# Seven places for split weights, and the first stick-breaking head loaded through ScalarE's queue

## The chip, the cores and the metric

The kernel runs on one core of one Trainium2 chip. The metric is device time in microseconds (us). TensorE (PE) multiplies, VectorE (DVE), ScalarE (ACT) and GpSimd (POOL) do the elementwise work, and SyncE (SP) issues nearly all DMAs. "PEld" is PE's weight load, which the profile lists apart from the matmul.

## The reference, cut to what matters

One layer of a hybrid encoder is computed for 1024 prompt tokens and 32 streaming tokens (with 512 cached positions), model width 1024, all in float32:

```python
z = einsum(rmsnorm(x), w_in)            # q/k/v of mixers A and B, indexer, two gates
o_a = softmax over the 256 best keys    # mixer A: 8 heads of 64, top-k by a small indexer
a   = exp(log_sigmoid(z) - tail)        # mixer B: stick-breaking, strictly causal, 8 heads of 64
m   = sigmoid(gate_a) * (o_a @ w_branch_a) + sigmoid(gate_b) * (o_b @ w_branch_b)
h   = x + m @ w_out
y   = h + relu(rmsnorm(h) @ w_up)**2 @ w_down
```

The new keys and values of both mixers are outputs too.

## The kernel before, in words

**Split numbers.** A float32 product is made of three matmuls of the type fp32r: each operand is split into a high part and the rest, and `three` issues high by high, high by rest, rest by high. A weight block of 128x512 is a *unit*: SP loads it into one of three places `wst`, ACT rounds it into `wh` (a CAST), and POOL or DVE subtracts to get `wl`. The pairs `wh0/wl0`, `wh1/wl1` and so on are the *places for split weights*; `unit` and, in the feed-forward part, `form` take them in turn (`self.place = (self.place + 1) % WB`). A place can be written again only when PE has read the unit that was in it before.

**Stages.** (1) RMS norm and the indexer's projections; (2) the projections of mixer B (`project_b`) and the indexer's scores, with the top-k search by bits on DVE and ACT beside them; (3) the projections of mixer A (`project_a`): for each of four pairs of heads a value part, whose columns go to bank `pj`, are scaled by DVE into `vt` and transposed by PE, and a query/key part, nine tiles of tokens in banks `s` and `pj`, which DVE rotates; (4) stick-breaking attention, eight heads (`attend(h, False)`); (5) softmax attention in two passes; (6) merge, output projection and feed-forward network (a Strassen scheme), from about 890 us on to the end.

**One head of stick-breaking attention.** `attend` loads k, q and v from DRAM, where the projections left them. For each of eight tiles of 128 queries it multiplies k and q into a bank `s` (three of them), ACT takes two sigmoids of it (`p` and `rem`), DVE scans `rem`, POOL multiplies `p` by it, PE transposes `p` into a bank `t` (two), ACT and DVE split that into `tt`, and PE multiplies `tt` by v into a bank `o`.

**What sets the order.** Nothing is issued in the order in which it is written. Every operation is recorded, and a planner (`Plan`) plays them through with a table of costs: an engine that falls free takes the operation of the best rank whose inputs are there by these costs, and the order thus found is fixed for each engine. The ranks are FAST (evictions), PREP (loads and splits), MAIN, FILL and SLOW. Matmuls of weights have rank FILL (`with nc.rank(FILL)`): the projections of the gates and, later, of the branches are there to fill PE while attention waits for ACT, DVE and POOL. On the chip each engine runs its list in order and waits by semaphores. Operations recorded as `nc.either` go to DVE or POOL, whichever the planner finds earlier done. All recorded operations are issued from one line, 440, so groups are told apart by their tiles' names.

**The place of the change.** After `project_a` the pool `att` is opened in the memory of the closed pools, and three gates are recorded before the first head. `nc.tile(pool, shape, type, name, bufs=n)` gives the n places of a name in turn, and a place lies where the pool stands when it is first asked for. So the order of the first requests decides which older tile lies beneath, and what must end before the place is written.

Of the kernel before, what the change touches and what calls it, by code (L numbers as in the profile page):

```python
# [10 lines left out]
F32 = mybir.dt.float32  # L11
F32R = mybir.dt.float32r
# [11 lines left out]
SEQ = 1024  # L24
# [16 lines left out]
LS = PAST + DEC  # L41
W1 = 512
NEW = 8
WB = 5
MIDS = 1
FILL_AHEAD = 1
GATES_BEFORE, GATES_FIRST = 4, 3
# [17 lines left out]
def cut(L):  # L65

    return L // 2 if L in (640, LS) else 512
# [392 lines left out]
class Layer:  # L460
# [21 lines left out]
    def unit(self, src):  # L482
# [5 lines left out]
        with nc.rank(PREP):  # L488
            st = nc.tile(self.wpool, [128, 512], F32, "wst", bufs=3)
            h, l = (nc.tile(self.wpool, [128, 512], F32R, f"{z}{self.place}") for z in ("wh", "wl"))  # L490
            self.place = (self.place + 1) % WB
            nc.sync.dma_start(st, src)
# [71 lines left out]
    def run(self):  # L564
        nc, a = self.nc, self.a
# [12 lines left out]
        w = lambda *x: [nc.tile(self.wpool, [128, 512], F32R, name) for name in x] and None  # L578
# [11 lines left out]
        w("wh3", "wl3")  # L590
        self.fq = s([128, NT, H], "fq")
        w("wh4", "wl4")
        with nc.rank(PREP):
            nc.scalar.dma_start(self.gm, a["g_mix"])
        nc.vector.memset(self.rs, 1.0)
# [4 lines left out]
        dt = lambda shape, name: nc.tile(self.dram, shape, F32, name)  # L600
# [62 lines left out]
        self.low = nc.either  # L663
        self.att = self.pr = nc.open("att", "right")
        self.first = nc.tile(self.att, [128, T], U8, "first")
        nc.gpsimd.memset(self.first[:, DEC:SEQ + DEC - 128], 0)
        nc.scalar.copy(self.first[:, :DEC], self.eye4)
        nc.scalar.copy(self.first[:, SEQ + DEC - 128:], self.ident)
# [405 lines left out]
            nc.sync.dma_start(self.fqs[32 * j:32 * j + 32], self.fq[:DEC, NEW, j::4])  # L1074


    def rope_tables(self):
        nc, a, pr = self.nc, self.a, self.pr
        self.tc_ = nc.tile(pr, [128, NT, 2, HD], F32, "tabc")
        self.ts_ = nc.tile(pr, [128, NT, 2, HD], F32, "tabs")  # L1080
        C = nc.tile(pr, [128, NT, HD], F32, "ropec")
        S = nc.tile(pr, [128, NT, HD], F32, "ropes")
        g = nc.tile(pr, [128, 2, HD], F32, "gqk")
        nc.sync.dma_start(C, a["rope_c"])
        nc.sync.dma_start(S, a["rope_s"])
        nc.sync.dma_start(g, a["g_qk"].unsqueeze(0).to_broadcast([128, 2, HD]))
        for j in range(2):
            nc.gpsimd.tensor_mul(self.tc_[:, :, j], C, g[:, j].unsqueeze(1).to_broadcast([128, NT, HD]))
            gx = g[:, j].rearrange("p (s e) -> p s e", s=2)[:, ::-1, :].unsqueeze(1).to_broadcast([128, NT, 2, 32])
            nc.gpsimd.tensor_mul(  # L1090
                self.ts_[:, :, j].rearrange("p t (s e) -> p t s e", s=2),
                S.rearrange("p t (s e) -> p t s e", s=2), gx)
# [161 lines left out]
    def attend(self, h, is_a, passes=(0, 1)):  # L1254

        nc, at = self.nc, self.att
        g = h if is_a else H + h
        direct = is_a and passes[0] == 1 and h >= H - 2
        if direct and h == H - 2:
            self.last = nc.tile(at, [128, SEQ], F32, "last", tag="v", bufs=3)  # L1260
        kk = nc.tile(at, [128, SEQ], F32R, "k", bufs=3)
        v = nc.tile(at, [128, 8, 128], F32R, "v", bufs=3)
        dk = self.dk[g].rearrange("s e t -> (s e) t")
        qs = {}
        for i in range(passes[-1] + 1):
            nc.sync.dma_start(kk.bitcast(F32)[:, 512 * i:512 * i + 512], dk[:, 512 * i:512 * i + 512])
            if i in passes:
                qs[i] = nc.tile(at, [128, 2, 512], F32R, "q", bufs=2)
                for s in range(2):
                    nc.sync.dma_start(  # L1270
                        qs[i].bitcast(F32)[HD * s:HD * s + HD],
                        self.dq[g].rearrange("s e t -> e s t")[:, :, 512 * i:512 * i + 512])
            nc.sync.dma_start(v.bitcast(F32)[:, 4 * i:4 * i + 4], self.dv[g, :, 4 * i:4 * i + 4])

        def weights(t, q, *room):
            L = 128 * (t + 1)
            qh, ql = (q[:, s, t % 2 * 128:t % 2 * 128 + 128] for s in range(2))
            parts = []
            for c0 in range(0, L, cut(L)):
                n = min(cut(L), L - c0)  # L1280
                ps = self.bank("s")
                nc.tensor.matmul(ps[:, :n], qh, kk[:, c0:c0 + n], start=True, stop=False)
                nc.tensor.matmul(ps[:, :n], ql, kk[:, c0:c0 + n], start=False, stop=True)
                parts.append((c0, ps[:, :n]))
            if is_a:
                return self.softmax_weights(parts, L, self.mask[t], self.fq[:, t, h:h + 1], room[0])
            return self.stick_weights(parts, L, *room, self.first[:, DEC + SEQ - L:][:, ::-1])

        for i in passes:
            o = nc.tile(at, [64, 512], F32, "o", bufs=2)  # L1290
            for t0 in (4 * i + 2, 4 * i):
                c = 128 * (t0 - 4 * i)
                q = qs[i][:, :, c:c + 256]
                if i:
                    pw = [weights(t, q, *self.rooms(is_a)) for t in (t0, t0 + 1)]
                else:
                    room = self.rooms(is_a)
                    pw = [weights(t0 + j, q, *(z[:, 512 * j:512 * j + 512] for z in room)) for j in range(2)]
                po = self.bank("o")[:, :256]
                for j0 in range(0, t0 + 2, 2):  # L1300
                    pt = self.bank("t")
                    blocks = [(j, u) for j in (j0, j0 + 1) for u in range(2) if j <= t0 + u]
                    for m, (j, u) in enumerate(blocks):
                        nc.tensor.transpose(
                            pt[:, m * 128:m * 128 + 128], pw[u][:, j * 128:j * 128 + 128], self.ident)
                    parts = self.split_pt(pt, 128, 128 * len(blocks))
                    for j in (j0, j0 + 1):
                        lo = 128 if j > t0 else 0
                        s0 = 256 * (j - j0)
                        for z in range(2):  # L1310
                            nc.tensor.matmul(
                                po[:, lo:256], v[:, j], parts[:, z, s0:s0 + 256 - lo],
                                start=j + z == 0, stop=j + z == t0 + 2)
                self.halves(po, o[:, c:c + 256], self.last[h % 2 * HD:h % 2 * HD + HD, c:c + 256] if direct else None)
            if not direct:
                with nc.rank(FAST):
                    nc.sync.dma_start(self.do[g, :, 512 * i:512 * i + 512], o)
            self.mid = self.mid[1:] + [len(nc.nodes) - 1]
# [248 lines left out]
    def ffn(self, rp):  # L1567
# [13 lines left out]
        def form(x, n=512):  # L1581
            with nc.rank(PREP):
                h, l = (nc.tile(self.wpool, [128, 512], F32R, f"{z}{self.place}") for z in ("wh", "wl"))
                self.place = (self.place + 1) % WB
                h, l = h[:, :n], l[:, :n]
# [109 lines left out]
    def down(self, late, form):  # L1695
# [87 lines left out]
        for (fs, weights, after), b, block in (  # L1783
# [4 lines left out]
            total, ask = len(fs) * len(block), iter(range(len(fs) * len(block)))  # L1788
            runs = [block] if len(fs) > 1 else [block[:8], block[8:]]
            for run, q in [(run, q) for run in runs for q in range(4)]:  # L1790
                if q not in banks:
                    tags = [next(self.turn) for _ in fs]
# [130 lines left out]
```

## Time and profile before

| | us |
|---|---|
| three runs | 1676.88, 1678.47, 1678.60 |
| median | 1678.47 |
| the profiled execution's own time | 1679.89 |
| its span, first to last instruction | 1678.1 |
| PE busy in it | 1663.3 (99%) |
| PE loading weights | 1587.8 (95%) |
| DVE, ACT, POOL busy | 1355.1, 945.1, 804.2 |

Matmuls overlap in PE, so each one's duration in the profile is longer than its share of the time: a matmul of 512 columns is listed with about 0.40 us, while the next one starts 0.23 us later. What a matmul costs is the distance between two starts. A number in brackets behind a row, with an arrow, is idle time of the engine just before that row, and who ended it. TensorE's granted clock is 1.00 in every stretch of this section's profile. The chain of waits is PE for 84% of the span.

### The profile page before, as it was taken

How to read it: one execution, taken by the hardware profiler on the slowest of the kernel's cores; microseconds unless marked ns; L12 is line 12 of the kernel's file. 1: busy time of each engine (PE TensorE's matmuls, PEld its weight loads, DVE VectorE, ACT ScalarE, POOL GpSimd, SP SyncE). 2: the span in 40 equal slices, each digit the busy share in tenths (PEclk: the TensorE clock that was granted, in tenths of full speed). 3: DMA queues.
4: the chain of work that ended last, by engine and by line, in shares of the span. 5: the costliest groups of instructions: out<-in, count | busy, mean ns of one | idle time of the engine just before them, and what ended most of it. 6: DMA issues, size and time to landing. Idle time of an engine off the chain costs nothing.

```text
span 1678.1 us, 34748 instructions
## 1 busy us (share of the span) xinstructions
PE 1663.3 (99%) x12244; PEld 1587.8 (95%) x12244; DVE 1355.1 (81%) x2830; ACT 945.1 (56%) x2008; POOL 804.2 (48%) x681
## 2 busy tenths in 40 slices
PE   9999999999999999999999999999999999999999
PEld 9898999899989999998989999999999999999999
DVE  6777899987579889887877649998988997678775
ACT  7556888764366768886665545333333453443431
POOL 4532332344356576354556348544433466345564
PEclk9999999999999999999999999999999999999999
DMA  8243454355573636788764644444444596676674
GB/s 284 61 125 107 142 185 144 99 155 148 163 218 103 181 100 178 190 264 247 227 188 142 178 123 134 157 146 142 142 142 135 198 326 223 204 232 200 222 227 137
DMA packets 182126, 290.31 MB, mean 173 GB/s; under 512 B 29472, under 2 KB 61696, under 8 KB 181920
## 3 DMA queue, kind: packets, MB, share of 16 engines
q1 hardware_dynamic: 181664, 287.91, 55.1%
q8 instruction: 97, 1.59, 0.4%
q14 instruction: 77, 0.63, 0.1%
q10 hardware_dynamic: 288, 0.17, 0.0%
HBM read 195.09 MB, written 94.90 MB: 173 GB/s over the span
## 4 chain that ended last, share of the span: by engine, by line
PE 84%; DVE 7%; DMA 4%; ACT 2%; issue 2%; POOL 1%; SPq 1%; DVEq 0%; ACTq 0%; POOLq 0%
PE pj L440 34%; PE c L440 11%; PE a L440 11%; PE b L440 11%; PE s L440 9%; PE o L440 4%; PE t L440 4%; DVE junk L440 2%; DMA xt<-x 1%; SPq L440 1%; DVE qi L440 0%; DVE y L440 0%; DMA q<-dq 0%; DMA kl<-dc 0%; DVE ta L440 0%
## 5 line engine op out<-in xcount | busy, mean ns | idle before, releaser
L440 PE MATMUL pj<-xl,wh 128*128 128x272 f32 (+2 forms) x1200 | 334.0, 312 | 0.0
L440 POOL TENSOR_TENSOR wl<-wst,wh 128x512 fp32r<-128x512 f32 x125 | 175.4, 1408 | 219.4 <-ACT wh L440 192.9
L440 PE MATMUL pj<-xh,wh 128*128 128x272 f32 (+1 forms) x768 | 251.7, 328 | 0.0
L440 PE MATMUL pj<-xh,wl 128*128 128x272 f32 (+1 forms) x768 | 250.6, 326 | 0.2 <-POOL wl L440 0.2
L440 PEld LDWEIGHTS pj<-xl,wh 128*128 128x128 f32 x1200 | 212.7, 188 | 10.0
L440 ACT CAST wh<-wst 128x512 fp32r<-128x512 f32 x197 | 120.7, 619 | 126.6 <-PE pj L440 35.0
L440 PEld LDWEIGHTS pj<-xh,wl 128*128 128x128 f32 x768 | 144.6, 188 | 10.8 <-POOL wl L440 0.5
L440 PEld LDWEIGHTS pj<-xh,wh 128*128 128x128 f32 x768 | 144.6, 188 | 10.1 <-DVE gz L440 0.3
L440 POOL TENSOR_TENSOR p<-p,rem 128x383 f32<-128x383 f32 (+8 forms) x66 | 107.2, 1639 | 64.7 <-DVE rem L440 31.1
L440 ACT CAST wh<-us 128x512 fp32r<-128x512 f32 x80 | 49.7, 621 | 122.6 <-PE pj L440 34.3
L440 DVE TENSOR_TENSOR tt<-t,tt 128x512 fp32r<-128x512 f32 (+2 forms) x168 | 100.2, 620 | 16.8 <-ACT tt L440 16.0
L440 DVE TENSOR_TENSOR_SCAN rem<-rem,first 128x384 f32<-128x384 f32 (+8 forms) x66 | 107.2, 1642 | 2.0 <-ACT rem L440 1.6
L440 POOL TENSOR_TENSOR wl<-y,wh 128x512 fp32r<-128x512 f32 x46 | 68.6, 1492 | 77.7 <-ACT wh L440 74.7
L440 ACT ACTIVATE junk<-score,cand 128x1024 bf16<-128x1024 f32 (+2 forms) x93 | 96.9, 1042 | 12.5 <-DVE cand L440 11.0
L440 ACT CAST wh<-y 128x512 fp32r<-128x512 f32 x79 | 49.0, 621 | 96.8 <-PE c L440 20.5
L440 ACT CAST tt<-t 128x512 fp32r<-128x512 f32 (+2 forms) x168 | 85.8, 540 | 27.5 <-PE t L440 18.5
L440 PE MATMUL o<-tt,v 128*128 128x256 f32 (+1 forms) x640 | 98.5, 279 | 0.5 <-DVE o L440 0.5
L440 PE MATMUL s<-k,q 128*128 128x512 f32 (+4 forms) x384 | 98.2, 351 | 0.7 <-DMA q<-dq 0.7
L440 PEld LDWEIGHTS o<-tt,v 128*128 128x128 f32 x640 | 90.5, 189 | 6.1 <-DVE o L440 1.1
L440 DVE TENSOR_SCALAR_CACHE_REDUCE junk<-score,cand 128x384 bf16<-128x384 f32 (+1 forms) x124 | 92.9, 749 | 3.1
L440 PE MATMUL t<-ident,p 128*128 128x128 f32 (+1 forms) x596 | 90.7, 275 | 0.0
L440 POOL TENSOR_SCALAR p<-p,nb 128x384 f32<-128x384 f32 (+6 forms) x66 | 53.5, 817 | 70.8 <-DVE nb L440 59.6
(401 smaller groups left out, 5624.3 us busy)
## 6 DMA issues: line engine op xcount, KB each, us to landing
us<-w_down SPq DMA_DIRECT2D x80, 256.0 KB, 3.3
q<-dq SPq DMA_DIRECT2D x64, 256.0 KB, 4.1
du<-us SPq DMA_DIRECT2D x56, 264.0 KB, 2.7
du<-y SPq DMA_DIRECT2D x56, 264.0 KB, 3.0
y<-w_up SPq DMA_DIRECT2D x44, 256.0 KB, 2.8
k<-dk SPq DMA_DIRECT2D x40, 256.0 KB, 4.1
v<-dv SPq DMA_DIRECT2D x40, 256.0 KB, 4.0
xl<-du SPq DMA_DIRECT2D x35, 264.0 KB, 4.7
```

The source lines that it names most:

```text
L440: fn(*args, **kw)
```

## The change

The number of places for split weights goes from five to seven (`WB`), so two more pairs of 128x512 are taken from the pool `w`. When the pool `att` is opened, all places of six of its names are now asked for at once, in a fixed order. And the loads of k, q and v of stick-breaking head 0 (two loads of k, four of q, two of v) are issued by ACT instead of SP.

```diff
-WB = 5
+WB = 7
...
         w("wh4", "wl4")
+        for i in range(5, WB):
+            w(f"wh{i}", f"wl{i}")
...
         self.first = nc.tile(self.att, [128, T], U8, "first")
+        self.places(self.att, [
+            ("gz", [128, 512], F32, 3), ("rem", [128, SEQ], F32, 4), ("tt", [128, 2, 512], F32R, 4),
+            ("v", [128, 8, 128], F32R, 3), ("k", [128, SEQ], F32R, 3), ("q", [128, 2, 512], F32R, 2)])
...
+    def places(self, pool, tags):
+
+        for name, shape, dt, n in tags:
+            for _ in range(n):
+                self.nc.tile(pool, shape, dt, name, bufs=n)
...
         dk = self.dk[g].rearrange("s e t -> (s e) t")
+        load = (nc.sync if h or is_a else nc.scalar).dma_start
         qs = {}
         for i in range(passes[-1] + 1):
-            nc.sync.dma_start(kk.bitcast(F32)[:, 512 * i:512 * i + 512], dk[:, 512 * i:512 * i + 512])
+            load(kk.bitcast(F32)[:, 512 * i:512 * i + 512], dk[:, 512 * i:512 * i + 512])
...
-                    nc.sync.dma_start(
+                    load(
...
-            nc.sync.dma_start(v.bitcast(F32)[:, 4 * i:4 * i + 4], self.dv[g, :, 4 * i:4 * i + 4])
+            load(v.bitcast(F32)[:, 4 * i:4 * i + 4], self.dv[g, :, 4 * i:4 * i + 4])
```

PE has the same 12,235 matmuls in both kernels. Their order is the same up to the 508th, in the index stage, and from there on the planner, which sees more room for units, finds another one on every engine. Three places matter here.

**Start of stick-breaking attention, PE.** `s<-k,q` are the scores of head 0, `t<-ident,p` its transposes, `pj<-..,wh` and `..,wl` the matmuls of gates. Before:

```order
L440 MATMUL s<-k,q 128x384 x2
L440 MATMUL s<-k,q 128x512 x2
L440 MATMUL s<-k,q 128x128 x2
L440 MATMUL pj<-xh_106,wh_4209 128x272
L440 MATMUL pj<-xl_107,wh_4209 128x272
```

Nine gate matmuls stand there, then the scores of the 256-column tile, then nine matmuls of the next gate, and only then the transposes. Now:

```order
L440 MATMUL s<-k,q 128x384 x2
L440 MATMUL s<-k,q 128x512 x2
L440 MATMUL s<-k,q 128x128 x2
L440 MATMUL s<-k,q 128x256 x2
L440 MATMUL s<-k,q 128x512
L440 MATMUL t<-ident,p 128x128 x2
L440 MATMUL s<-k,q 128x512
L440 MATMUL s<-k,q 128x384 x2
L440 MATMUL s<-k,q 128x512 x2
L440 MATMUL t<-ident,p 128x128 x5
L440 MATMUL s<-k,q 128x512 x2
L440 MATMUL o<-tt,v 128x256
```

The gate's last nine matmuls now stand ahead of the first scores, and no gate matmul stands between the first scores and the first product with v.

**The same place, ACT.** Now ACT issues the loads of head 0 in its own list:

```order
L440 CAST first<-ident 128x128
L440 DMA k<-dk 128x512
L440 DMA q<-dq 64x2x512 x2
L440 DMA v<-dv 128x512
L440 ACTIVATE gz<-gz 128x512
L440 DMA k<-dk 128x512
L440 DMA q<-dq 64x2x512 x2
L440 DMA v<-dv 128x512
L440 ACTIVATE gz<-gz 128x272 x2
L440 ACTIVATE p<-s 128x384
```

Before, these eight stood in SP's list, and the two CASTs of the next gate's unit stood right behind the first two sigmoids; now the first such CAST comes behind eleven sigmoids and a CAST of `tt`:

```order
L440 ACTIVATE p<-s 128x512
L440 ACTIVATE rem<-s 128x512
L440 ACTIVATE p<-s 128x384
L440 CAST tt<-t 128x512
L440 CAST wh_6371<-wst 128x512
```

**End of mixer A's projections, PE.** `pj<-xl,wh` with 272 columns are the last value columns of a pair, `t<-ident,vt` their transposes, `pj<-wh,xh` with 256 columns a tile of tokens of the query/key part. Now:

```order
L440 MATMUL pj<-xl_111,wh_4076 128x272
L440 MATMUL pj<-xh_110,wl_4077 128x272
L440 MATMUL t<-ident,vt 128x128 x2
L440 MATMUL t<-ident,vt 32x128
L440 MATMUL pj<-wh_4089,xh_110 128x256
```

and, 24 matmuls later, `t<-ident,qk 128x128 x4` and at once the first `pj` matmul of a gate. Before, the tile of tokens ahead of those four transposes was one of bank `s`, and the transposes of `vt` stood further from the matmuls that make them. So a transpose of `vt` now follows directly on the last matmul whose result DVE scales for it.

**Second pass of softmax attention, PE.** `pj<-og` are matmuls of a branch. Now:

```order
L440 MATMUL t<-ident,p 128x128 x8
L440 MATMUL pj<-og,wl_7521 128x512
L440 MATMUL o<-tt,v 128x256 x5
L440 MATMUL t<-ident,p 128x128 x2
L440 MATMUL o<-tt,v 128x256 x3
L440 MATMUL t<-ident,p 128x128 x5
L440 MATMUL o<-tt,v 128x256 x2
L440 MATMUL o<-tt,v 128x128 x2
```

Before, ten or eight branch matmuls stood between such transposes and their products:

```order
L440 MATMUL t<-ident,p 128x128 x6
L440 MATMUL pj<-og,wh_7497 128x512 x2
L440 MATMUL pj<-og,wl_7498 128x512
L440 MATMUL pj<-og,wh_7497 128x512 x2
L440 MATMUL pj<-og,wl_7498 128x512
L440 MATMUL pj<-og,wh_7497 128x512 x2
L440 MATMUL o<-tt,v 128x256
```

The branch matmuls between transposes and products have shrunk from eight to one, and to none further on.

## The prediction, made before the changed kernel was run

> **What bounds the kernel now.** I read the page's busy times first, then engine busy times by stretch, the waits of ACT by releaser, and last PE's timeline wherever an idle time stands in brackets. In a stretch's row the columns are start and end, length, busy us of PE, PE's weight load, DVE, ACT and POOL with instruction counts, granted clock, DMA share and GB/s.
>
> ```profile
> span 1678.1 us, 34748 instructions
> PE 1663.3 (99%) x12244; PEld 1587.8 (95%) x12244; DVE 1355.1 (81%) x2830; ACT 945.1 (56%) x2008; POOL 804.2 (48%) x681
> ...
> 280.00:425.00 145.00, 142.43 (x1088) 135.35 (x1087) 124.62 (x355) 91.49 (x194) 60.42 (x60) 1.00 0.48 138
> 1040.00:1390.00 350.00, 350.00 (x2877) 350.00 (x2876) 316.70 (x533) 143.87 (x311) 159.74 (x109) 1.00 0.51 175
> ...
> ACT wh L440 <- PE pj L440: 87.0, 57, 4.0
> ACT wh L440 <- PE c L440: 68.7, 43, 2.4
> ```
>
> PE is idle for 1678.1 - 1663.3 = 14.8 us in all. No faster preparation can give back more than that, and the matmuls stay the same. In the feed-forward stretch, 1040 to 1390, PE has no gap at all. The last two rows, the largest of their kind, show what two more places for split weights attack: ACT waits 87.0 and 68.7 us until PE has read the old unit. That is much, but it is ACT's time (56% busy). A unit ready earlier than PE wants it earns nothing. So more places gain only where PE itself waits for a split, and there is little of that. What the change does instead is indirect: the planner finds another order, and the time is set by whether that order still covers the few chains through ACT, DVE and POOL.
>
> **The change part by part.**
>
> *Seven places, in the feed-forward part and the gates' units:* 0. The cover is PE's own work, 350.00 of 350.00 above; the bound below is 0 too, since nothing can be gained there. If the cover were gone, a unit would cost ACT's cast and the subtraction, and that would show as PE behind `wl`.
>
> *Start of stick-breaking attention.* Before, PE looked like this:
>
> ```profile
> 468.70 1.15 PE L440 MATMUL s<-k,q 128*128 128x384 f32 x6
> 469.69 0.34 PE L440 MATMUL pj<-xh,wh 128*128 128x272 f32 x1
> ...
> 470.87 0.40 PE L440 MATMUL s<-k,q 128*128 128x256 f32 x2
> 471.10 0.39 PE L440 MATMUL pj<-xh,wh 128*128 128x512 f32 x1
> ...
> 471.80 0.28 PE L440 MATMUL pj<-xl,wh 128*128 128x272 f32 x1
> 472.32 0.50 PE L440 MATMUL pj<-xh,wl 128*128 128x512 f32 x1 [0.24 <-POOL wl L440]
> ...
> 473.96 0.48 PE L440 MATMUL pj<-xh,wl 128*128 128x512 f32 x1
> 475.18 1.52 PE L440 MATMUL s<-k,q 128*128 128x512 f32 x6 [0.74 <-DMA q<-dq]
> 476.54 0.39 PE L440 MATMUL pj<-xh,wh 128*128 128x512 f32 x1
> ```
>
> Two waits: 472.32 - 471.80 = 0.52 where 0.12 is usual (0.40 lost), and 475.18 - 473.96 = 1.22 where 0.23 is usual (0.99 lost, for the second half of q). Everything else is filled with gate matmuls. In the new order all of the gate's matmuls are ahead of the first score, and up to the first product with v there are only scores and transposes. Their chain, from rows of before:
>
> ```profile
> 469.25 0.49 ACT L440 ACTIVATE p<-s 128x384 f32<-128x384 f32 x1 [1.34 <-PE s L440]
> 469.64 0.49 ACT L440 ACTIVATE rem<-s 128x384 f32<-128x384 f32 x1
> 470.01 1.15 ACT L440 CAST wh<-wst 128x512 fp32r<-128x512 f32 x2
> ...
> 470.23 0.96 DVE L440 TENSOR_TENSOR_SCAN rem<-rem,first 128x384 f32<-128x384 f32 x1 [0.36 <-ACT rem L440]
> ...
> 472.24 1.31 POOL L440 TENSOR_TENSOR p<-p,rem 128x383 f32<-128x383 f32 x1
> ...
> 478.62 0.71 PE L440 MATMUL t<-ident,p 128*128 128x128 f32 x5
> 479.08 0.54 PE L440 MATMUL s<-k,q 128*128 128x320 f32 x2
> ```
>
> The first sigmoid starts 469.25 - 468.70 = 0.55 after the first score, the scan at 470.23 - 468.70 = 1.53 and ends at 2.49. A hand-over takes 0.10 (`rem` ends at 470.13, the scan starts at 470.23). So POOL's product of 1.31 ends at 3.9, and the first transposes start at about 4.0. PE's work ahead of them is 0.99 (469.69 - 468.70, six scores) + 0.23 + 0.23 = 1.45. Then it goes on at the pace of ACT, which reads the banks `s` (three of them) in turn: the second half of the 512-column tile at 4.4, ACT's sigmoids of that tile from 4.6 and 5.1, the next `p` at 5.6, a cast of `tt` at 6.0, and only behind that, in ACT's list, the cast of the next gate's unit, which (1.15 for two, 0.6 for one) lets the first gate matmul start at about 7.2, with `tt` 0.59 ahead of it. PE's work up to there: 0.99 + 0.23 + six scores of 512 1.36 (476.54 - 475.18) + two of 384 0.34 + seven transposes 0.76 (five take 0.46 above with one score's start; 0.109 each by my estimate) + one product 0.12 = 3.8. So PE waits 7.2 - 3.8 = 3.4, and the two old waits (1.4) go: **+2.0**. Bounds: +0.5, if the second tile's scan and product hide fully in the first's (1.5 less), and the upper one under the loads below. A gain here is excluded, since 4.0 - 1.45 = 2.55 up to the first transposes alone is more than 1.4.
>
> *The loads through ACT.* Before, SP issued them, the second half of q behind stores and other loads (a piece of the chain of waits, two of SP's issues, a sigmoid of ACT, a stretch):
>
> ```profile
> 467.89 7.15 DMA q<-dq
> ...
> 466.45 0.42 SPq L440 DMA_DIRECT2D k<-dk  x1
> 466.93 1.57 SPq L440 DMA_DIRECT2D q<-dq  x2
> ...
> 464.72 0.63 ACT L440 ACTIVATE gz<-gz 128x512 f32<-128x512 f32 x1 [4.91 <-DVE gz L440]
> ...
> 466.00:476.00 10.00, 9.03 (x57) 7.76 (x57) 6.28 (x11) 5.13 (x14) 3.53 (x3) 1.00 1.03 319
> ```
>
> ACT is idle 4.91 us ahead of that sigmoid, so issuing the first four loads costs nothing (k 0.42, two of q 1.57, and v at most the 0.79 of a q: 2.8 us). The second four stand behind the sigmoid, which waits for DVE in the new list too. The second q can go out at 464.72 + 0.63 + 0.42 + 0.79 = 466.56, and with the same 7.15 us lands at 473.7 instead of 475.04. The first score now comes 470.87 - 469.69 = 1.18 later, at 469.88; counted from it, that is 3.8, just inside the 4.0 that PE waits anyway. Price: 0 in the sum. If it lands no earlier than before, 475.04 - 469.88 = 5.2, PE waits 1.2 more, which gives the upper bound of +3.2. In that stretch the DMA share is 1.03: the transfers already fill all engines, so an earlier issue need not be an earlier landing.
>
> The Trainium skill, page "DMA: Bandwidth & Descriptors", section "Issuing engines are not separate DMA queues", says that DMAs issued by ScalarE, SyncE and GpSimd run on the same 16 DMA engines and interleave, and that several issuers save only the issue time. The share of 1.03 agrees; by that rule the loads gain at most their place behind SP's other issues, and the sum would be the one with +3.2.
>
> *End of mixer A's projections.* PE's waits of before:
>
> ```profile
> 296.63 0.38 PE L440 MATMUL s<-wh,xh 128*128 128x256 f32 x1 [0.36 <-ACT sq L440]
> ...
> 311.70 0.36 PE L440 MATMUL s<-wh,xh 128*128 128x256 f32 x1 [0.17 <-DVE cand L440]
> ...
> 324.64 0.36 PE L440 MATMUL s<-wh,xh 128*128 128x256 f32 x1 [0.23 <-DVE tb L440]
> ...
> 334.91 0.24 PE L440 MATMUL t<-ident,qk 32*128 32x32 f32 x1 [1.06 <-DVE az L440]
> ...
> 339.50 0.27 PE L440 MATMUL t<-ident,vt 128*32 128x128 f32 x1 [0.23 <-DVE small L440]
> ...
> 415.16 0.38 PE L440 MATMUL s<-wh,xh 128*128 128x256 f32 x1 [0.37 <-ACT wh L440]
> ```
>
> Their brackets sum to 2.4 (PE's whole idle time from 280 to 425 is 145.00 - 142.43 = 2.57); the true loss is some 0.16 more each (as 0.24 against 0.40 above), 3.4. The one of 1.06 stays: its transposes are as close behind their rotation as before. So 2.2 go. New are three transposes of `vt` directly on the last matmul of their columns. And twice a `pj` matmul of 256 columns wants a bank from which DVE has still to read two products. DVE's part:
>
> ```profile
> 467.01 0.44 DVE L440 TENSOR_TENSOR gz<-pj,rb 128x272 f32<-128x272 f32 x1 [2.32 <-PE pj L440]
> ...
> L440 DVE TENSOR_TENSOR ta<-pj,tabc x12: 386/412/425, 298.1 to 432.7; 128x256 f32<-128x256 f32 x12
> ```
>
> A transpose of `vt` waits for the end of a 272-column matmul (0.34 listed), DVE's scaling (0.44, the row's for as many columns, an estimate for `vt`) and the hand-over 0.10, less the usual 0.12: 0.75. A `pj` matmul waits 0.36 + 2 x 0.41 + 0.10 less four transposes (0.44) and 0.12, that is 0.7. New 3 x 0.75 + 2 x 0.7 = 3.6, gone 2.2: **+1.4**. Lower bound +0.2 (DVE's part half hidden: 5 x 0.24 less), upper +3.8 (all five as bad as the worst of before, 1.2 each, less 2.2).
>
> *At about 690 us* ACT's list has two function-table loads ahead of a pair of casts:
>
> ```profile
> L440 ACT ACT_TABLE_LOAD x6 | 7.7, 1283 | 0.1
> ```
>
> Their number is about that of before, but these two, 1.28 each, stand just ahead of a unit that PE wants; nothing in the trace of before shows it. Between 0 (unit ready) and one load, 1.3, I take the middle, **+0.6**.
>
> *Second pass of softmax attention, about 870 us.* Eight transposes have one branch matmul (0.23) behind them, then products:
>
> ```profile
> 847.28 0.52 PE L440 MATMUL s<-kl,qz 128*128 128x272 f32 x2 [0.65 <-POOL kl L440]
> ...
> L440 ACT CAST tt<-t 128x512 fp32r<-128x512 f32 x51 | 29.1, 592 | 7.1 <-PE t L440 5.6
> L440 DVE TENSOR_TENSOR tt<-t,tt 128x512 fp32r<-128x512 f32 x100 | 66.9, 681 | 8.7 <-ACT tt L440 8.1
> ```
>
> ACT's 0.59 and DVE's 0.68 give 1.27 less 0.23, so some 1.0 where nothing else is in flight; then two shorter groups of which half is covered, 0.5 each: 2.0. Against that, the wait for `kl` (0.65, with the 0.16 and a smaller second one about 1.0) goes, since its copy on POOL is now planned earlier: **+1.0**, between 0 (the products are of a tile split earlier) and 2.0 (kl still waits).
>
> **Sum:** 2.0 + 1.4 + 0.6 + 1.0 = +5.0 on the profiled execution's 1679.89 gives 1684.9. That execution is 1.42 above the median of the runs, 1678.47, so the median becomes 1683.5. For places in the new order that I have not priced I add nothing and allow 1.5 either way.
>
> **The rivals.**
> - *Not slower, even faster.* The new order could cover its chains: PE's list puts a transpose or product where the planner's costs have the input ready, and those costs may simply be right. Place: transposes of `vt`, `qk` and the second pass. Point of decision: whether DVE's scaling ends before the matmul ahead of the transpose does. Then the three later terms are -2.2, 0 and -1.0; if also only the first part of the attention's start counts (+0.5), the median is 1678.47 - 2.7 = 1675.8; with the full +2.0, 1677.3. With the start covered as well (against it: no gate matmul stands there) it is 1678.47 - 1.4 - 3.2 = 1673.9. Chance 0.33: 0.10 of faster, 0.23 of within.
> - *The change does not do what it says.* The second half of q lands as late as before, because the transfers share the engines (DMA share 1.03): +1.2, so 1684.7. For it: 7.15 us is the slowest of q's landings. Against: the loads are no longer behind SP's stores. Chance 0.14.
> - *The clock drops.* Every row above has granted clock 1.00. The first matmuls of the program show what cold costs:
>
> ```profile
> 1.19 4.21 PE L440 MATMUL t<-warm 128*128 128x128 f32 x18 [1.19 <-DVE warm L440]
> ```
>
> 0.234 each against 0.109. If 2.5 us of waiting at the start of attention sufficed, some 2.5 us of work behind it would take twice as long: 1686.0. Against: the stretch is broken by scores. Chance 0.05. The Trainium skill, page "TensorE: Matmul & The Clock Gate", section "Part 1: The HAM clock gate", tells of such a gate; the row agrees in kind, and no row here shows a drop once warm.
>
> **How the numbers follow.** The forecast's case has 0.48. A measurement of this kernel can hardly tell less than 0.2%, 3.4 us, from no change: 1675.1 to 1681.8 counts as the same. Of the forecast's case about 0.07 lies under 1681.8 (by the lower bounds 0.5 + 0.2 + 0 + 0, 1679.2). Faster 0.10; same 0.23 + 0.07 = 0.30; slower 0.41 + 0.14 + 0.05 = 0.60. Its own range is 1679 to 1688; with the covered order, whose better half starts at 1675.8, and the upper bounds (3.2 + 3.8 + 1.3 + 2.0 = +10.3, 1688.8, hardly all at once) the range is 1676 to 1689.
>
> **What would show it.** Right: PE idle at the first head's start with releasers `p` on POOL and `s` or `rem` on ACT, 3 us or more between the first score and the first gate matmul not filled; transposes of `vt` waiting 0.6 or more for DVE; a bracket of about 1 behind `tt` near 870; PE's busy time of 1040 to 1390 unchanged. Wrong: PE's total idle time under 15 us, or a wait for q still the largest at that place, or a granted clock under 1.00 near 470, or a difference inside the feed-forward part, where I price nothing.

## The result and the profile after

The changed kernel takes 1699.35 us (median of 4 runs, 1698.70 to 1701.54), the kernel before 1678.40 beside it. The ratio is 1.013 with a 95% interval of 1.0114 to 1.0146: 21 us slower, where +5 was forecast and 1689 was the upper end of the range. The direction was right and the size wrong by a factor of four.

The profiled execution took 1699.98 us, its span is 1696.8, 18.7 more than before. The first lines of its page:

```profile
span 1696.8 us, 34711 instructions
PE 1669.5 (98%) x12244; PEld 1592.2 (94%) x12244; DVE 1369.8 (81%) x2846; ACT 948.0 (56%) x2008; POOL 783.9 (46%) x665
```

PE is idle for 1696.8 - 1669.5 = 27.3 us instead of 14.8, which makes 12.5 of the 18.7. The other 6.2 are PE time: the same 12,244 instructions are busy for 1669.5 instead of 1663.3 us. How they divide was not measured, but the rows show two things. A matmul that stands ahead of a wait counts with its whole listed length, and PE waits more often. And where the granted clock is 0.50 (last section), PE issues 7 matmuls in a us instead of 10.

Busy times by stretch, first of the kernel before, then of the changed one (start and end, length, PE, PE's weight load, DVE, ACT, POOL, granted clock, DMA share, GB/s):

```profile
280.00:440.00 160.00, 157.43 (x1192) 149.18 (x1191) 134.88 (x379) 98.32 (x210) 68.70 (x68) 1.00 0.47 136
440.00:520.00 80.00, 78.73 (x519) 71.67 (x517) 54.21 (x87) 46.17 (x111) 37.12 (x26) 1.00 0.58 170
680.00:840.00 160.00, 159.81 (x1131) 149.02 (x1131) 128.96 (x424) 126.52 (x264) 72.64 (x81) 1.00 0.81 237
840.00:960.00 120.00, 118.96 (x781) 108.66 (x781) 88.20 (x181) 67.55 (x141) 66.81 (x63) 1.00 0.58 169
```

```profile
280.00:440.00 160.00, 153.47 (x1168) 145.72 (x1167) 128.97 (x367) 96.83 (x205) 68.25 (x67) 1.00 0.47 134
440.00:520.00 80.00, 75.77 (x470) 68.16 (x470) 53.10 (x84) 44.00 (x98) 37.92 (x24) 0.96 0.57 166
680.00:840.00 160.00, 157.40 (x1104) 145.67 (x1103) 129.61 (x404) 122.56 (x262) 71.44 (x79) 1.00 0.75 223
840.00:960.00 120.00, 117.06 (x795) 107.70 (x794) 93.23 (x200) 72.75 (x147) 66.76 (x60) 1.00 0.61 186
1040.00:1390.00 350.00, 348.69 (x2856) 347.79 (x2855) 326.24 (x563) 141.34 (x308) 145.39 (x99) 1.00 0.50 170
```

PE's idle time grows from 2.57 to 6.53 us at the end of mixer A's projections, from 1.27 to 4.23 at the start of stick-breaking attention (with a mean clock of 0.96), from 0.19 to 2.60 at the start of softmax attention, from 1.04 to 2.94 behind it. Even the feed-forward stretch has lost 1.31.

The start of attention, PE and ACT of the changed kernel:

```profile
473.80 1.15 PE L440 MATMUL s<-k,q 128*128 128x384 f32 x6
477.73 0.80 PE L440 MATMUL s<-k,q 128*128 128x256 f32 x2 [2.77 <-ACT rem L440]
478.98 0.76 PE L440 MATMUL s<-k,q 128*128 128x512 f32 x1 [0.46 <-ACT rem L440]
480.62 0.69 PE L440 MATMUL t<-ident,p 128*128 128x128 f32 x2 [0.87 <-POOL p L440]
480.96 2.27 PE L440 MATMUL s<-k,q 128*128 128x512 f32 x5
...
485.06 0.50 PE L440 MATMUL pj<-xh,wh 128*128 128x512 f32 x1
```

```profile
465.58 1.32 ACTq L440 DMA_DIRECT2D q<-dq  x2
470.12 0.34 ACTq L440 DMA_DIRECT2D v<-dv  x1
470.50 0.63 ACT L440 ACTIVATE gz<-gz 128x512 f32<-128x512 f32 x1 [5.15 <-DMA q<-dq]
...
471.57 1.81 ACTq L440 DMA_DIRECT2D q<-dq  x2
475.80 0.33 ACTq L440 DMA_DIRECT2D v<-dv  x1
476.17 0.75 ACT L440 ACTIVATE gz<-gz 128x272 f32<-128x272 f32 x2 [5.03 <-DMA q<-dq]
476.82 0.47 ACT L440 ACTIVATE p<-s 128x384 f32<-128x384 f32 x1
```

From the first score to the first gate matmul it is 485.06 - 473.80 = 11.26 us, not 7.2. ACT's first sigmoid starts 3.02 after the first score, not 0.55: it stands in ACT's list behind loads that ACT could not issue. The issue of v waited from 466.9 to 470.12, the last one from 473.4 to 475.80.

The brackets of those rows put both waits down to q. The landings say otherwise: the first two loads of q landed at 472.1 and 472.8, some 2 us after v had gone out. The first v went out 0.1 us behind the landing of a store that SP had issued (`dg<-gz`, issued at 463.74, landed 6.3 us later), the second directly behind the landing of the second k (issued at 471.21, landed 4.6 us later). In the trace each of these two issues waits for the semaphore of that earlier DMA. The bracket of 0.46 has a similar error: the second half of q was issued at 472.80 and landed 6.0 us later, at 478.8, so that the score at 478.98 was held up by q to the end, and not by ACT.

### The profile page after: what moved, and what is told of

It is laid out like the page before. It is cut to its first block, busy times and chain, and to the rows that moved or that the text cites. A ratio compares the mean times of both kernels' runs of the same rounds, so it can differ in the third digit from the quotient of the medians.

```text
span 1696.8 us, 34711 instructions
## 1 busy us (share of the span) xinstructions
PE 1669.5 (98%) x12244; PEld 1592.2 (94%) x12244; DVE 1369.8 (81%) x2846; ACT 948.0 (56%) x2008; POOL 783.9 (46%) x665
## 5 line engine op out<-in xcount | busy, mean ns | idle before, releaser
L440 POOL TENSOR_TENSOR wl<-wst,wh 128x512 fp32r<-128x512 f32 x115 | 166.3, 1450 | 159.1 <-ACT wh L440 134.9
L440 POOL TENSOR_TENSOR p<-p,rem 128x127 f32<-128x127 f32 (+8 forms) x66 | 104.6, 1600 | 90.2 <-DVE p L440 37.1
L440 DVE TENSOR_TENSOR_SCAN rem<-rem,first 128x128 f32<-128x128 f32 (+8 forms) x66 | 110.9, 1698 | 2.3 <-ACT rem L440 1.5
L440 DVE TENSOR_TENSOR wl<-wst,wh 128x512 fp32r<-128x512 f32 x82 | 75.2, 919 | 15.8 <-ACT wh L440 15.2
L440 POOL TENSOR_SCALAR p<-p,nb 128x384 f32<-128x384 f32 (+6 forms) x66 | 49.9, 761 | 75.0 <-DVE nb L440 56.9
```

What stands on the lines that cost most here:

```text
L440: fn(*args, **kw)
```

## The experiments

All times are told as the difference to the kernel before, measured beside each.

**1. The same order, with SP issuing head 0's loads.** The planner still counts them as ACT's.

```diff
+        self.head0 = Issuer(self, ACT, nc.sync)
-        load = (nc.sync if h or is_a else nc.scalar).dma_start
+        load = (nc.sync if h or is_a else nc.head0).dma_start
```

> The changed kernel with one edit: the eight loads of head 0 are still planned as ScalarE's, so every list of PE, ACT, DVE and POOL keeps the changed order, but SP issues them. Theory 'blocked ScalarE': in the changed kernel ACT stands still about 5 us twice at these issues, its first sigmoid starts 3.0 us after the first score's start instead of 0.55, and PE's idle stretch of up to 3 us at that place is followed by 8 us at a granted clock of 0.6 to 0.7; without ACT's issues 4 to 7 us come back, near 1693.5, and the granted clock at 475 to 485 us is 1.00 again. Rival 'the order alone': the transposes wait for the chain through DVE and POOL anyway, and less than 1 us comes back, 1698.5 to 1699.5.

Measured: 1700.91 against 1679.24, ratio 1.0129 (1.0112 to 1.0146). Nothing came back; the theory of the blocked ScalarE fails as the cause of the 21 us. In the stretch itself:

```profile
476.95 0.47 ACT L441 ACTIVATE p<-s 128x384 f32<-128x384 f32 x1
```

```profile
480.78 0.76 PE L441 MATMUL s<-k,q 128*128 128x512 f32 x1 [2.42 <-DMA q<-dq]
...
485.82 0.69 PE L441 MATMUL pj<-xh,wh 128*128 128x512 f32 x1
```

The first score is at 475.94 here, so the sigmoid comes 1.0 behind it instead of 3.0. But now q is late, and PE waits 2.42 for it. First score to first gate matmul is 9.88, 1.4 less than in the changed kernel, and the clock still drops. The order leaves PE nothing else to do, whichever of the two obstacles comes first. (The 1.4 us are not seen in the whole: between 680 and 840 us this run's PE is idle 5.13 us against 2.60, with the same order; the last section comes back to that.)

**2. The order of before, with ACT issuing head 0's loads** (the reverse edit, `Issuer(self, SP, nc.scalar)`).

> The kernel before with one edit: its order on PE, ACT, DVE and POOL is kept, but the eight loads of head 0 are issued by ACT, as in the changed kernel. Theory 'blocked ScalarE': ACT stands still at the issues, the first sigmoids come late, and the gate's matmuls cover only a part: 2 to 4 us slower than before, 1680.5 to 1682.5. Rival 'harmless issue': within 0.7 us of before, since ACT is idle there.

Measured: 1680.47 against 1679.24, ratio 1.0005 (0.9996 to 1.0014): no difference that can be told. Issued by ACT, the loads cost nothing in this order. The run tests a blocked ACT only in part, though. The longest that an issue waits is about 2 us (a load of q, from 464.2 to 466.17), ACT's idle times there (4.91, 2.29 and 2.58 us) are put down to DVE and PE, and the first sigmoid starts 1.95 us after the first score instead of 3.02.

**3. Seven places alone** (`WB = 7`, no `places`, loads on SP).

> Seven places for split weights alone, with the loads on SP and the places in the order of first requests. Theory 'the order that seven places bring': the waits for vt and for bank pj between 280 and 440 us (4.7 us more than before), and those from 680 us on, are all there; 11 to 15 of the 21 us, 1689 to 1693. Rival 'the loads are the cause': under 5 us slower than before, below 1683.5. My recorded sum without its first term would give 1681.5.

Measured: 1691.02 against 1679.24, ratio 1.0069 (1.0054 to 1.0084), +11.8 us. Up to the start of attention its PE list is that of the changed kernel, and PE is busy 153.46 of the 160 us from 280 to 440, as there.

**4. Everything but the two places more** (`WB = 5`).

> The changed kernel with five places for split weights instead of seven: the loads on ACT and the places asked for at once stay. Order up to 440 us is then that of before. Theory 'the order that seven places bring' for the most part, and the blocked ScalarE at the start of attention for the rest: 5 to 9 us slower than before, 1683.5 to 1687.5, all of it behind 440 us. Rival 'the loads are the cause': 15 us or more slower.

Measured: 1686.32 against 1679.24, ratio 1.0041 (1.0026 to 1.0056), +7.1 us. By these two runs the parts nearly add up, 11.8 + 7.1 = 18.9. PE's idle time shows where the second part lies: 2.75 us from 440 to 520 (1.27 before) and 2.64 from 840 to 960 (1.04 before). Experiment 11 takes up whether it is the loads.

**5. Seven real places in the order of before.** Each unit gets one of seven places, but the planner is also told to wait for the unit five before it.

```diff
+                ring = self.rings.setdefault((pool[3], "like " + like), [])
+                m.also = ring[-1].touched if ring else ()
+                ring.append(m)
...
+                    deps.update(m.also)
```

> Seven real places for split weights, while the planner counts as if a unit had to wait for the one five before it: the order on every engine is that of the kernel before, row for row. Theory 'the loss is the order, not the room': within 1 us of before, and ACT's waits for PE's reads shrink without any gain in time. Rival 'the room itself costs' (other addresses, other waits): 3 us or more slower. Rival 'the room itself gains': 2 us or more faster.

Measured: 1679.80 against 1679.48, ratio 1.0003 (0.9994 to 1.0013). ACT's waits for PE's reads:

```profile
ACT wh L446 <- PE c L446: 21.1, 10, 2.3
...
ACT wh L446 <- PE pj L446: 18.3, 10, 2.4
```

They fall from 87.0 to 18.3 behind `pj` and from 68.7 to 21.1 behind `c`, and the time stays. (In the trace the rows of PE, ACT and POOL come in the same order as before.) In this order the room neither gains nor costs. What costs is the order. In the changed kernel, with its own order, the same two waits hardly fall: 78.6 and 58.8.

**6. The idle time filled.** Twenty matmuls, whose results are overwritten, are put between the first scores and transposes; all lists are otherwise those of the changed kernel.

```diff
+FILLED = {0: 11, 1: 3, 6: 6}
...
+            for _ in range(n):
+                self.tc.nc.tensor.matmul(self.first_t[:, :512], q, k[:, :512], start=True, stop=True)
```

> The changed kernel, its order kept on all engines, with 20 additional matmuls of 512 columns (4.5 us of work) put into PE's idle time at the first head's start; they write a bank that the transposes behind them overwrite. Theory 'the idle time lowers the clock, and that costs more': the granted clock stays 1.00 from 470 to 490 us, and the stretch from the first score to the first product with v shrinks from 10.8 to about 9 us; the whole 1.5 to 2.5 us faster than the changed kernel, about 1697. Rival 'the clock costs nothing beside the waits': the stretch stays 10.5 or more, or grows by the added work, 1699 to 1701.

Measured: 1701.46 against 1679.48, ratio 1.0127 (1.011 to 1.0144). The stretch 475 to 485, of the changed kernel and of this one:

```profile
475.00:485.00 10.00, 5.87 (x18) 4.32 (x18) 5.10 (x10) 5.93 (x16) 4.25 (x4) 0.66 1.04 350
```

```profile
475.00:485.00 10.00, 8.71 (x42) 6.29 (x41) 5.98 (x12) 6.70 (x18) 4.26 (x4) 1.00 1.06 333
...
483.67 0.38 PE L442 MATMUL o<-tt,v 128*128 128x256 f32 x1
484.18 0.50 PE L442 MATMUL pj<-xh,wh 128*128 128x512 f32 x1
```

The idle time does lower the clock, and 4.5 us of extra work keep it at 1.00. But the first product with v comes 10.26 after the first score (473.41) instead of 10.83, and the first gate matmul 10.77 instead of 11.26. So the work in the gap gains about 0.5 us, not 2: most matmuls of this stretch wait for ACT, POOL or q anyway. The 0.5 is net, because the last six extra matmuls stand ahead of the first transposes and hold them up, though the first `p` was there at 479.9: the transposes come 7.61 us after the first score instead of 6.82. From the first transposes to the first product with v it is 2.65 us instead of 4.01. By these rows the low clock itself costs between 0.5 and about 1.4 us here.

**7. and 8. One nanosecond in the planner's table**, in the kernel before and in the changed one.

```diff
-SLACK, STORE, LEAN = 300, 1000, 500
+SLACK, STORE, LEAN = 301, 1000, 500
```

> The kernel before with one number of the planner's cost table changed by one nanosecond (300 to 301 for the hand-over between engines): five places, loads on SP, but the planner finds another order from some point on. Theory 'any new order loses, since the old one was picked among many': 4 us or more slower, 1683 or more. Rival 'seven places bring worse orders than five': within 2.5 us of before.

> The changed kernel with the same one nanosecond in the planner's cost table: another order of the same kind. The transposes of vt right behind their matmuls at 285 to 345 us and the late oa near 1535 us stay in its order; the one at 430 us and the uncovered transposes near 890 us do not. Theory 'seven places bring worse orders, of which the changed kernel's is one': 1690 to 1697, still 11 us or more over before. Rival 'the 21 us are one bad draw': under 1687.

Measured: 1679.06 against 1679.48 (ratio 0.9997, 0.9988 to 1.0007) with five places, and 1688.46 against 1679.48 (ratio 1.0055, 1.004 to 1.007) for the changed kernel, +9.0 instead of +21 us. The result lies between what the two theories of 8 said: a good half of the loss came with this one order, 9 us did not go away.

**9. Shorter counting passes on DVE**, the order kept.

```diff
+            if SHORT[0] <= self.counts < SHORT[1]:
+                args[:2] = [z[:, :32] for z in args[:2]]
```

> The changed kernel, its order kept, but the last 20 counting passes of the top-k search on DVE (from about 299 us on) read 32 columns instead of 384 to 640: some 0.2 us each instead of 0.6 to 0.9. It leaves out most of these counts, so the last bits of the search are not found. Theory 'the transposes of vt wait for DVE's queue': at 306.7 us the scaling of vt stands behind such passes, and its transposes wait 1.6 us; with short passes that wait falls to about 0.75 and the one behind (1.7 us, DVE's split after a pass of 0.77) to about 1.0, while the wait of 1.4 at 342.6, behind another operation, stays. Rival 'only the chain itself, matmul to scaling to transpose': the waits stay within 0.2 us.

In the changed kernel PE and DVE stood so:

```profile
306.67 0.28 PE L440 MATMUL pj<-xh,wl 128*128 128x272 f32 x1
308.39 0.55 PE L440 MATMUL t<-ident,vt 128*128 128x128 f32 x3 [1.43 <-DVE vt L440]
...
311.46 0.28 PE L440 MATMUL pj<-wh,xl 128*128 128x256 f32 x1
313.28 0.63 PE L440 MATMUL t<-ident,qk 128*128 128x128 f32 x4 [1.55 <-DVE vs L440]
```

```profile
307.21 0.77 DVE L440 TENSOR_SCALAR_CACHE_REDUCE junk<-score,cand 32x544 bf16<-32x544 f32 x1
...
307.91 0.42 DVE L440 TENSOR_TENSOR vt<-pj,rb 128x272 f32<-128x272 f32 x1
```

With short passes:

```profile
306.26 0.29 PE L446 MATMUL pj<-xh,wl 128*128 128x272 f32 x1
307.09 0.55 PE L446 MATMUL t<-ident,vt 128*128 128x128 f32 x3 [0.53 <-DVE vt L446]
...
310.15 0.28 PE L446 MATMUL pj<-wh,xl 128*128 128x256 f32 x1
311.05 0.63 PE L446 MATMUL t<-ident,qk 128*128 128x128 f32 x4 [0.62 <-DVE vs L446]
```

Measured: start to start, 1.72 becomes 0.83 for `vt` and 1.82 becomes 0.90 for `qk`; the wait at 342.6 stays. The span is 2.0 us shorter (1694.8), and the ratio to before 1.0101 (1.0086 to 1.0116). So the larger half of these waits was DVE's queue: the scaling of `vt` takes 0.42, but a pass of 0.77 stood ahead of it, and more in front of that.

**10. Six places alone.**

> Six places for split weights alone, loads on SP. Theory 'each place more makes the order worse, mostly where the planner fills': between five and seven, 2 to 8 us slower than before, 1681.5 to 1687.5; waits for vt or qk at 285 to 345 us and the oa wait of 2.1 us near 1530 us are there as with seven. Rival 'seven is a bad draw, six is not': within 1.5 us of before.

Measured: 1683.54 against 1679.46, ratio 1.0024 (1.0015 to 1.0034), +4.1 us. The wait for `vt` at 307 us is there, the late `oa` is not: PE waits there no longer than before.

**11. Experiment 4 with one nanosecond more** (`SLACK` 301).

> Five places with the loads planned on ACT and the places asked for at once, with one nanosecond more in the planner's hand-over cost. The same kernel without that nanosecond was 7 us slower than before. Theory 'a bad draw behind the start of attention': the waits near 883 and 886 us change, those at the start (2.5 us) stay, 2 to 5 us slower than before. Rival 'the loads cost it': 6 us or more slower.

Measured: 1680.19 against 1679.46, ratio 1.0006 (0.9996 to 1.0015). The whole is 0.7 us slower, where experiment 4 was 7.1. Neither the theory's 2 to 5 nor the rival's 6 came out, so most of the seven microseconds were the luck of one order. The start of attention did not become cheap: ACT stands still for 10.00 us there, the first sigmoid starts 2.6 us after the first score, and PE is idle 3.04 us from 440 to 520 (2.75 in experiment 4). That is made up for elsewhere, from 280 to 440 us for instance (1.3 instead of 2.6).

**12. The kernel before with 20 ns more** (`SLACK` 320).

> The kernel before with 20 ns more in the planner's hand-over cost (300 to 320): five places, loads on SP, another order. Theory 'any new order can lose some us': 2 to 6 us slower than before. Rival 'five places are robust': within 1.5 us of before, as with one nanosecond.

Measured: 1685.73 against 1679.46, ratio 1.0033 (1.0019 to 1.0046), +6.3 us. Five places have bad orders too.

**13 to 16. Three more orders with seven places, one with five.** What was open is whether seven places are worse as such.

> Seven places alone, loads on SP, one nanosecond more in the planner's hand-over cost. Theory 'seven places give worse orders': 7 to 11 us slower than before (the waits for vt and qk at 285 to 345 us, 3 us more than before, and the late oa at 1530 us stay, others come and go). Rival 'luck of one order': under 3 us slower.

> Seven places alone, loads on SP, ten nanoseconds more in the planner's hand-over cost. Theory 'seven places give worse orders': 9 to 15 us slower than before. Rival 'luck of one order': under 3 us slower.

> Seven places alone, loads on SP, twenty nanoseconds more in the planner's hand-over cost. Theory 'seven places give worse orders': 6 to 12 us slower than before. Rival 'luck of one order': under 3 us slower.

> The kernel before with ten nanoseconds more in the planner's hand-over cost: five places, loads on SP. Theory 'seven places give worse orders than five': within 3 us of before, and clearly under the three orders with seven places. Rival 'luck of one order': anywhere up to 10 us slower.

Measured: 1687.97, 1698.28 and 1691.43 against 1679.11 with seven (ratios 1.0051, 1.0112, 1.0065; intervals 1.0034 to 1.0068, 1.0096 to 1.0128, 1.005 to 1.008), and 1678.41 with five (0.9996, 0.9987 to 1.0006). All orders that were measured, whoever issued head 0's loads, with PE's idle time from 280 to 440 us read from the same stretch as above:

| places | difference to before, us (PE idle 280 to 440, us) |
|---|---|
| five | 0 (2.6), -0.4 (1.3), -0.7 (2.9), +0.7 (1.3), +6.3 (3.1), +7.1 (2.3) |
| six | +4.1 (3.3) |
| seven | +8.9 (5.0), +9.0 (5.0), +11.8 (6.5), +12.3 (3.5), +19.2 (8.1), +21.0 (6.5) |

The rival of luck alone is hard to hold: no order with seven places came under +8.9, none with five over +7.1. The twelve are not twelve independent draws, though: with each number of places, two pairs share PE's list up to the first scores of head 0. All come from small steps of one planner number; whether other numbers would suit seven places better was not tried. Luck is the other half: with the same places, orders differ by 8 us (five) and 12 us (seven).

The four pairs that share PE's list up to there also show what the other part of the change does. One of each pair has the loads of head 0 on ACT and the places asked for at once, the other neither:

| pair | difference to before, us, without and with | PE idle 440 to 520, us, without and with |
|---|---|---|
| before, 4 | 0, +7.1 | 1.27, 2.75 |
| 7, 11 | -0.4, +0.7 | 2.22, 3.04 |
| 13, 8 | +8.9, +9.0 | 2.36, 3.36 |
| 3, changed kernel | +11.8, +21.0 | 2.18, 4.23 |

At its own place this part costs PE 0.8 to 2.1 us of idle time in all four pairs. What it adds to the whole lies between 0.1 and 9.2 us, by the order that comes with it. The issuer alone makes no difference that can be told (experiments 1 and 2); the places asked for at once were not tested by themselves.

No kernel beat the one before. Why the planner's orders are worse with more room was not settled. But their traces share two waits. For `vt`, PE waits 1.40 to 2.39 us near 308 us in all six orders with seven places and 1.81 us with six, and in none with five. For `oa`, near 1530 us, it waits 1.69 to 2.38 us with seven places and 0.97 to 1.34 us with five.

## Why the prediction was right and wrong, point by point

- **More places gain nothing by themselves: right.** The two waits of ACT that the prediction quotes fell to a quarter in experiment 5 (155.7 to 39.4 us together), and the time stood still.
- **The loss is the order: right in kind, and it was looked for at the right places.** Every term of the sum has the right sign.
- **Start of attention, +2.0: mis-sized.** The path from first score to first gate matmul was 11.26 instead of 7.2. Less PE's 3.8 and the old waits of 1.4 that makes +6.1. The step that failed is "The loads through ACT", priced at 0 because ACT is idle there. The price counted the time of each issue (0.4 to 0.8) and not that an issue can itself wait; behind it stood the sigmoids, 2.5 us later than priced. Nor would SP have helped: then q is late (experiment 1), and first score to first gate matmul is still 9.88. A late q was the second rival, held at 0.14, and its price (1.2) was half of the wait found (2.42). Issued by ACT, the second half of q landed 5.0 us after the first score; the prediction gave 3.8, and 5.2 for this rival. The low clock has its share too (0.5 to 1.4, experiment 6).
- **End of mixer A's projections, +1.4: mis-sized, +4.2.** Removed were 2.2, as said. But the new waits were 1.60 + 1.42 + 0.70 + 0.36 for `vt`, 1.70 for `qk` behind `vs`, 1.25 + 0.58 for banks: 7.6 instead of 3.6, of which 1.2 replaces the old one of 1.06. The failed step is the chain of a transpose: matmul, DVE's scaling of 0.44, hand-over. It assumed a free DVE, where the quoted row shows DVE busy 124.62 of 145.00 us. (The rival 'not slower' had made this its point of decision: whether DVE's scaling ends in time. It did not.) Experiment 9 took the queue away, and the wait became 0.71 (0.83 less 0.12), where the chain had said 0.75.
- **At about 690 us, +0.6: +1.5.** It came at 725 us, behind two function-table loads as described: PE waited 1.14 for `wh` and 0.32 for the subtraction behind it.

```profile
723.40 1.28 ACT L440 ACT_TABLE_LOAD   x1
...
725.03 1.12 ACT L440 CAST wh<-wst 128x512 fp32r<-128x512 f32 x2
```

```profile
725.68 0.50 PE L440 MATMUL pj<-xh,wh 128*128 128x512 f32 x1 [0.97 <-ACT wh L440]
```

- **Second pass of softmax attention, +1.0: +1.9.** Four waits of 1.15, 0.61, 0.63 and 0.48, less 0.95 for `kl`. The chain of 1.27 was right; the "two shorter groups" were hardly covered.

```profile
891.60 0.48 PE L440 MATMUL pj<-og,wl 128*128 128x512 f32 x1
892.97 0.39 PE L440 MATMUL o<-tt,v 128*128 128x256 f32 x1 [0.90 <-ACT tt L440]
893.70 0.75 PE L440 MATMUL o<-tt,v 128*128 128x256 f32 x4 [0.34 <-DVE tt L440]
```

- **Places not priced, 0 with 1.5 either way: about +5.** 18.7 - 6.1 - 4.2 - 1.5 - 1.9 = 5.0 stays for them. The largest:

```profile
691.90 0.39 PE L440 MATMUL o<-tt,v 128*128 128x256 f32 x1 [0.75 <-DVE o L440]
...
924.80 0.39 PE L440 MATMUL b<-xl,wl 128*128 128x272 f32 x1 [1.03 <-POOL wl L440]
...
1096.40 0.39 PE L440 MATMUL pj<-wh,sum 128*128 128x272 f32 x1 [0.80 <-DVE us L440]
...
1538.00 0.39 PE L440 MATMUL pj<-oa,wh 128*128 128x256 f32 x1 [1.96 <-POOL oa L440]
```

  The last of these is old for the most part; before, the same wait was this:

```profile
1520.71 0.39 PE L440 MATMUL pj<-oa,wh 128*128 128x256 f32 x1 [1.34 <-POOL oa L440]
```

  So 0.6 us of it are new, and the low clock behind it costs some 1.6 us more (last section). A whole new order had been treated as four edits and a symmetric remainder. Yet PE was idle for only 14.8 us before, so a new order could win little and lose much: the remainder should have been one-sided.
- **No gap in the feed-forward part: wrong, by about 1 us** (the row at 1096 us).
- **The clock, 0.05: it did drop**, twice, and cost less than assumed at the first place (0.5 to 1.4 by experiment 6, where 2.5 were priced). The second drop, some 1.6 us, came at a place that had no price.
- **The range** ended at 1689 because it added the upper bounds of the four terms (3.2 + 3.8 + 1.3 + 2.0) to the median. Three of the four were broken (6.1, 4.2, 1.5 and 1.9 came), and the 5.0 at places without a price had no room in it. Of the six orders with seven places, four lie above it.

## What to carry to other kernels

When an order comes from a planner, an edit that gives it more room is a new draw of the whole order: compare several draws (a nanosecond in a cost is enough) before an effect is ascribed to the edit, and test the room alone by keeping the old order. Price a wait on an engine that works through its list by what stands ahead in that list, not by the duration of the operation waited for. A load moved to a computing engine can hold up everything behind it for as long as its issue has to wait; count that, not the issue's own time.

## What the runs showed of the hardware that was not expected

**An idle time of 2 to 3 us can halve the clock for some microseconds, and need not.** The changed kernel, around its longest wait and around that for `oa` (1.96, the row above):

```profile
477.00:478.00 1.00, 0.27 (x1) 0.27 (x2) 0.28 (x2) 1.00 (x3) 0.00 (x0) 0.71 1.04 254
478.00:479.00 1.00, 0.54 (x3) 0.28 (x3) 1.00 (x3) 1.00 (x5) 0.18 (x1) 0.50 1.02 338
...
484.00:485.00 1.00, 0.93 (x5) 0.54 (x3) 0.48 (x1) 1.00 (x3) 0.00 (x0) 0.88 1.11 381
...
1539.00:1540.00 1.00, 1.00 (x7) 1.00 (x6) 1.00 (x1) 0.50 (x1) 1.00 (x2) 0.50 0.01 2
...
1543.00:1544.00 1.00, 1.00 (x10) 1.00 (x10) 0.37 (x2) 0.19 (x1) 0.00 (x0) 1.00 0.95 315
```

The granted clock is 0.50 for some 6.8 us at the first (from 477.4 on) and 3.4 us at the second (from 1539.0 on), where PE issues 7 matmuls in a us instead of 10. In experiment 1, which has the same order, the same wait for `oa` left the clock at 1.00:

```profile
1541.91 0.39 PE L441 MATMUL pj<-oa,wh 128*128 128x256 f32 x1 [1.92 <-POOL oa L441]
```

From this matmul to the first `b<-xl,wh` behind it 4.13 us pass here, 4.14 in experiment 6, also at a clock of 1.00, and 5.69 in the changed kernel. So that drop cost some 1.6 us. In the second kernel of 13 to 16 a still later `oa` (PE idle for 2.38 us from 1533.8 us on) left the clock at 1.00 too. In the profiled executions every order with six or seven places has a drop somewhere, of 3.4 or 6.8 us, and none with five places has one between 10 and 1670 us.

The Trainium skill, page "TensorE: Matmul & The Clock Gate", section "Part 1: The HAM clock gate", names an idle window of about 3.4 us, on a beat of its own, as what lowers the clock. The lengths of 3.4 and twice 3.4 us are in keeping with such a beat. That a whole window must be idle is not in keeping with these traces: the drops here came with idle times of 2.77 and 1.96 us. What share of idle time suffices, and whether the beat decides between two equal waits, no run here shows.

**The same order is not the same time.** Experiments 1 and 6 have the changed kernel's order behind 490 us, but PE was idle 5.13 and 5.46 us from 680 to 840 instead of 2.60. Which load or wait begins this was not traced. The clock differs as well: experiment 1 has a drop of 3.4 us at 315.7, where the changed kernel has none, and none behind `oa`.
